# One transfer instead of two or four for keys, values and rotary queries, and another price of transfers in the layout in time

## The chip, the cores and the metric

The kernel runs on one core of one Trainium2 chip. A core has a matrix engine (PE, with its weight loads shown as PEld), a vector engine (DVE), a scalar engine (ACT), a general engine (POOL) and a queue that issues transfers (SP). The transfers themselves are carried out by 16 DMA engines of the core. The metric is the device time of one execution in microseconds (us).

## The reference, cut to what matters

One inference step of a 2-layer encoder over 2048 prompt positions and 64 sample positions. Each layer projects the input, runs four groups of heads (A: banded softmax attention; B: latent attention whose queries and keys have a rotary part of 32; C: stick-breaking attention; M: attention over 256 memory tokens), normalises and gates the heads, and projects back. The two groups that matter most here read the whole past:

```python
def mla_keys(ckv, krope, lp):                       # group B
    kv = heads(ckv @ lp['b_wkv_b'], B_HEADS)
    k_nope = rms(kv[..., :B_NOPE], lp['b_kn_g'])
    kr = jnp.broadcast_to(krope[:, :, None, :], krope.shape[:2] + (B_HEADS, B_ROPE))
    return jnp.concatenate([k_nope, kr], -1), kv[..., B_NOPE:]
...
def stick_break(q, k, v, qpos, kpos):               # group C
    z = jnp.einsum('bqhd,bkhd->bhqk', q, k).astype(jnp.float32) * Dh ** -0.5
    mask = kpos[None, :] < qpos[:, None]
    log_1m = jnp.where(mask, jax.nn.log_sigmoid(-z), 0.0)
    tail = lax.cumsum(log_1m, axis=3, reverse=True) - log_1m
    w = jnp.where(mask, jnp.exp(jax.nn.log_sigmoid(z) + tail), 0.0)
    return jnp.einsum('bhqk,bkhd->bqhd', w.astype(v.dtype), v)
```

## The kernel before, in words

The 2048 positions are 16 tiles of 128, and the sample is a 17th tile. The tiles lie in three blocks (6, 6 and 5 tiles). A stream of projections (`p_stream`) and a stream of attention (`attention`) are written alternately. Every number is split in a high and a low part, so that one product is two or three matmuls. A projected tile is transposed and stored in DRAM tensors: queries in `d["QA"]` to `d["QM"]`, rotary queries in `d["QR"]`, keys and values in `d["KVA"]`, `d["KVB"]`, `d["KVC"]` (a prompt's, in runs of 4 tiles), `d["KVM"]` and `d["KVS.."]` (memory and sample, runs of 2 tiles). The attention stream reads them back a head at a time.

`load_kv` brings the keys and values of one head and one run into the tile `kv`, whose 128 partitions hold the high part (0 to 63) and the low part (64 to 127). In DRAM these two halves lie in two halves of the tensor, so that it issues one transfer for each, of 64 rows. A full run of 4 tiles is 64 rows of 4 KB for each half; there are five `kv` buffers. `load_q` brings in the queries of a pair of tiles; for group B it also brings the rotary part `qr`, four transfers of 32 rows each, from the three copies in `d["QR"]` (the first copy twice). There is one `qr` buffer. `qr_stack` stores a tile of rotary queries: the high and low part by one transfer, a second high part by another.

Nothing is issued as it is written. A class `Plan` records each operation with its dependencies, gives it a duration (`cost`), lays all out in time (`issue`), and writes each engine's instructions in the order of the start times that it found. So the figures in `cost` decide the order on all engines, and through the buffers also when a transfer can be issued. All transfers are issued by SP, in its order; SP waits in that order too. All recorded instructions carry the line number of `issue` (L291) in the profile, so that tiles' names must tell them apart.

Of the kernel before, what the change touches and what calls it, by code (L numbers as in the profile page):

```python
# [7 lines left out]
F32 = mybir.dt.float32  # L8
F32R = mybir.dt.float32r
# [36 lines left out]
class Plan:  # L46
# [86 lines left out]
    def cost(self, eng, method, outs, ins, kw):  # L133

        def cols(x):
            n = 1
            for k in list(x.shape)[1:]:
                n *= k
            return n

        def sbuf(x):
            return "PSUM" not in str(x.space)

        n = cols(outs[0])
        if eng == "PE":
            if method == "transpose" or kw.get("rhs") is None:
                return 110, 271
            n = cols(kw["rhs"])
            return max(0.46 * n + 1, 110), 170 + 0.53 * n
        if eng == "SP":  # L150
            size = 4 * outs[0].shape[0] * n if len(outs[0].shape) > 1 else 4 * n
            return 530, 2800 + size * 0.0072
        if eng == "DVE":
            if method == "tensor_tensor_scan":
                d = 150 + 2.2 * n
            elif n <= 16:
                d = 185 + (cols(ins[0]) if method == "tensor_reduce" else 0) * 0.85
            elif len(ins) > 1 and sbuf(ins[0]) and sbuf(ins[1]):
                d = 200 + 1.35 * n
            else:  # L160
                d = 150 + 1.05 * n
            return d - 80, d
        if eng == "ACT":
            d = 190 + 0.76 * n
            if self.is_ap(kw.get("scale")):
                d += 90
            if len(outs) > 1:
                d += 230
            return d - 100, d
        if method == "memset":  # L170
            d = 100 + n
        elif kw.get("op") is not None and "pow" in str(kw["op"]):
            d = 600 if n == 1 else 1050
        elif method == "tensor_scalar":
            d = 245 + 1.3 * n
        else:
            d = 200 + 1.75 * n
        return d - 30, d
# [5 lines left out]
    def issue(self, tc):  # L184
        import heapq
        ops, tiles = self.ops, self.tiles
        n = len(ops)
# [17 lines left out]
        at = [0.0] * n  # L205
# [12 lines left out]
                        return key  # L218
            return None

        now, done = 0.0, 0
        while done < n:
            moved = False
            for e in ready:
                while clock[e] <= now and ready[e]:
                    i = heapq.heappop(ready[e])
                    key = slot(i)
                    if key is not None:
                        parked[key].append(i)
                        continue  # L230
                    for x in ops[i][5]:
                        if x not in held:
                            k = tiles[x][0]
                            held.add(x)
                            free[k] -= 1
                            turn[k] += 1
                            if turn[k] < len(order[k]) and free[k] > 0:
                                for j in parked[k]:
                                    heapq.heappush(ready[ops[j][0]], j)
                                parked[k] = []  # L240
                    take, last = ops[i][6]
                    if e == "ACT":
                        t = self.table(ops[i][3])
                        if t and t != act:
                            act = t
                            take, last = take + 1300, last + 1300
                    start[i] = now
                    clock[e] = now + take
                    heapq.heappush(events, (now + take, 0, e, i))
                    heapq.heappush(events, (now + last, 1, e, i))  # L250
                    moved = True
                    break
            if moved:
                continue
            if not events:
                raise AssertionError(("plan", done, {k: (v[:3], [ops[j][0] for j in v[:3]]) for k, v in parked.items() if v}))
            now = events[0][0]
            while events and events[0][0] <= now:
                _, kind, e, i = heapq.heappop(events)
                if kind == 0:  # L260
                    if e == "PE":
                        for j in after[i]:
                            if ops[j][0] == "PE":
                                left[j] -= 1
                                if left[j] == 0:
                                    heapq.heappush(ready["PE"], j)
                    continue
                if kind == 1:
                    done += 1
                    for x in ops[i][5]:  # L270
                        uses[x] -= 1
                        if uses[x] == 0:
                            k = tiles[x][0]
                            held.discard(x)
                            free[k] += 1
                            for j in parked[k]:
                                heapq.heappush(ready[ops[j][0]], j)
                            parked[k] = []
                    for j in after[i]:
                        if e == "PE" and ops[j][0] == "PE":  # L280
                            continue
                        heapq.heappush(events, (now + (10 if ops[j][0] == e else self.LAG[ops[j][0]]), 2, e, j))
                    continue
                left[i] -= 1
                if left[i] == 0:
                    heapq.heappush(ready[ops[i][0]], i)
# [26 lines left out]
def hybrid_step(  # L313
# [29 lines left out]
    pj = pool("pj")  # L343
    at = pool("at")
# [48 lines left out]
    def dt(name, shape, dtype=F32):  # L393
        return dram.tile(shape, dtype, name=name, tag=name)
# [5 lines left out]
    def layer_dram(l):  # L400
        d = {}
        for b, tl in enumerate(blocks):
            d["QR", b] = dt(f"qr{l}_{b}", [3, 128, len(tl) * 128])
            for g in "ABCM":
                d["Q" + g, b] = dt(f"q{g}{l}_{b}", [2, 256, len(tl) * 128])
                d["G" + g, b] = dt(f"g{g}{l}_{b}", [128, len(tl), 256])
        for g in "ABC":
            d["KV" + g] = dt(f"kv{g}{l}", [2, NH, HD, (NT + 3) // 4, 2, 512])
        for s in ("SA", "SB", "SC", "M", "SM"):
            d["KV" + s] = dt(f"kv{s}{l}", [2, NH, HD, 2, 256])  # L410
        d["KR"] = dt(f"kr{l}", [128, NT * 128])
        d["KRS"] = dt(f"krs{l}", [128, 256])
        d["Y"] = {t: dt(f"y{l}_{t}", [128, 1024]) for t in range(NT + 1)}
        D[l] = d
# [343 lines left out]
    def qr_stack(src, dst):  # L758

        pt = ps_st.tile([128, 128], F32, name="ptqr")  # L760
        T.transpose(pt, src, ident)
        kt = pj.tile([128, 2, 128], F32R, tag="qrs", name="qrs", bufs=1)
        A.copy(out=kt[:, 0], in_=pt)
        sub_r(kt[:, 1], pt, kt[:, 0])
        Y.dma_start(out=dst[0:2].rearrange("a p t -> p a t"), in_=kt.bitcast(F32))
        Y.dma_start(out=dst[2], in_=kt[:, 0].bitcast(F32))

    def v_stack(src, dst):

# [20 lines left out]
    def small_T(src, n, tag):  # L790

        pt = ps_st.tile([128, n, 128], F32, name="pts")
        for k in range(n):
            T.transpose(pt[:, k, :], src[:, k * 128:(k + 1) * 128], ident)
        h = pj.tile([128, n, 128], F32R, tag=tag + "h", name=tag + "h", bufs=1)
        lo = pj.tile([128, n, 128], F32R, tag=tag + "l", name=tag + "l", bufs=1)
        A.copy(out=h, in_=pt)
        sub_r(lo, pt, h)
        return h, lo
# [563 lines left out]
    def load_kv(d, g, h, c, n, sample):  # L1363
        kv = at.tile([128, 2, 512], F32R, tag="kv", name="kv", bufs=5)
        if sample or g == "M":
            src = d["KV" + ("S" if sample else "") + g][:, h]
        else:
            src = d["KV" + g][:, h, :, c]
        for a in range(2):
            Y.dma_start(out=kv[64 * a:64 * a + 64, :, 0:n * 128].bitcast(F32), in_=src[a, :, :, 0:n * 128])  # L1370
        return kv
# [10 lines left out]
    def group_units(l, b, g):  # L1382
# [13 lines left out]
        def load_q(p):  # L1396
# [4 lines left out]
            Y.dma_start(out=p["q"][0:64, :, 0:w].bitcast(F32), in_=src)  # L1401
            Y.dma_start(out=p["q"][64:128, 0, 0:w].bitcast(F32), in_=src[:, 0])
            if g == "B":
                p["qr"] = at.tile([128, 256], F32R, tag="qr", name="qr", bufs=1)
                for e in range(4):
                    Y.dma_start(out=p["qr"][32 * e:32 * e + 32, 0:w].bitcast(F32),
                                      in_=d["QR", b][e % 3, h * 32:(h + 1) * 32, t0:t0 + w])

        for h in range(NH):
            start = []  # L1410
# [409 lines left out]
```

## Time and profile before

| what | value |
|---|---|
| median of 3 runs | 3264.21 us (3263.85 to 3267.9) |
| profiled execution | 3270.62 us, of which the span is 3268.8 us |
| PE busy | 3136.6 us (96%) |
| DVE, ACT, POOL busy | 82%, 60%, 46% |
| moved by the DMA engines | 558.95 MB, mean 171 GB/s |

The span runs from the first instruction to the last. A busy share of PE of 96% says that PE is hardly ever without work; the shares of the other engines are averages over stages. The DMA share is an average over 16 DMA engines.

### The profile page before, as it was taken

How to read it: one execution, taken by the hardware profiler on the slowest of the kernel's cores; microseconds unless marked ns; L12 is line 12 of the kernel's file. 1: busy time of each engine (PE TensorE's matmuls, PEld its weight loads, DVE VectorE, ACT ScalarE, POOL GpSimd, SP SyncE). 2: the span in 40 equal slices, each digit the busy share in tenths (PEclk: the TensorE clock that was granted, in tenths of full speed). 3: DMA queues.
4: the chain of work that ended last, by engine and by line, in shares of the span. 5: the costliest groups of instructions: out<-in, count | busy, mean ns of one | idle time of the engine just before them, and what ended most of it. 6: DMA issues, size and time to landing. Idle time of an engine off the chain costs nothing.

```text
span 3268.8 us, 75613 instructions
## 1 busy us (share of the span) xinstructions
PE 3136.6 (96%) x24486; PEld 3004.7 (92%) x24486; DVE 2678.8 (82%) x7977; ACT 1959.3 (60%) x5336; POOL 1512.6 (46%) x2353
## 2 busy tenths in 40 slices
PE   8999989999999999999999989999999999999899
PEld 7999889999999998999999888989999998998798
DVE  5787868998889689887878977899878888887984
ACT  4455646767665565566656765666646567655650
POOL 4664445765346246442444544476313544212562
PEclk9999999999999999999999999999999999999999
DMA  6655776644656666566566667744455766566545
GB/s 187 196 153 165 198 205 196 160 120 140 169 159 194 200 184 179 150 171 179 148 187 181 173 179 218 197 138 131 137 142 166 210 197 188 158 173 175 151 129 157
DMA packets 576123, 558.95 MB, mean 171 GB/s; under 512 B 70960, under 2 KB 478000, under 8 KB 575728
## 3 DMA queue, kind: packets, MB, share of 16 engines
q1 hardware_dynamic: 575728, 554.10, 60.2%
q8 instruction: 196, 3.21, 0.4%
q14 instruction: 199, 1.63, 0.2%
HBM read 378.21 MB, written 173.75 MB: 169 GB/s over the span
## 4 chain that ended last, share of the span: by engine, by line
PE 66%; DVE 14%; DMA 8%; issue 4%; ACT 4%; POOL 2%; SPq 2%; POOLq 0%; DVEq 0%; ACTq 0%
PE pp L291 35%; PE ps L291 10%; PE ot L291 8%; PE pt L291 7%; DVE wh L291 4%; DVE r L291 3%; DVE ph L291 2%; PE ob L291 2%; SPq L291 2%; PE ptk L291 1%; ACT s L291 1%; DMA kv<-kvA 1%; PE ptq L291 1%; PE ptx L291 1%; DVE s L291 1%
## 5 line engine op out<-in xcount | busy, mean ns | idle before, releaser
L291 PE MATMUL pp<-wh,xh 128*128 128x256 f32 (+1 forms) x9104 | 1805.5, 291 | 26.1 <-ACT ev L291 10.3
L291 PEld LDWEIGHTS pp<-wh,xh 128*128 128x128 f32 x9104 | 1436.3, 190 | 61.7 <-DVE wh L291 18.6
L291 PE MATMUL pp<-wh,xl 128*128 128x256 f32 (+1 forms) x4416 | 1236.7, 281 | 2.2 <-DVE xl L291 1.9
L291 PEld LDWEIGHTS pp<-wh,xl 128*128 128x128 f32 x4416 | 838.8, 190 | 7.7 <-DVE xl L291 3.9
L291 POOL TENSOR_SCALAR wh<-raw,gc 128x256 fp32r<-128x256 f32 (+1 forms) x848 | 470.5, 570 | 355.2 <-PE pp L291 292.4
L291 ACT CAST ph<-pt 128x512 fp32r<-128x512 f32 (+2 forms) x840 | 454.2, 551 | 289.0 <-PE pt L291 276.2
L291 DVE TENSOR_TENSOR ph<-pt,ph 128x512 fp32r<-128x512 f32 (+2 forms) x840 | 523.5, 633 | 112.6 <-ACT ph L291 108.4
L291 PE MATMUL ot<-ph,kv 128*128 128x256 f32 (+1 forms) x3232 | 579.6, 289 | 6.9 <-DVE ph L291 3.2
L291 PE MATMUL ps<-kv,qbuf 128*128 128x256 f32 (+3 forms) x2048 | 541.5, 361 | 27.0 <-DVE r L291 8.8
L291 PE MATMUL pt<-identr,s 128*128 128x128 f32 x3056 | 504.1, 274 | 23.4 <-ACT s L291 11.3
L291 DVE SCALAR_TENSOR_TENSOR wh<-raw,gc,wh 128x256 fp32r<-128x256 f32 (+1 forms) x848 | 477.0, 596 | 24.6 <-POOL wh L291 21.9
L291 ACT ACTIVATE s<-s,nm 128x512 f32<-128x512 f32 (+4 forms) x600 | 383.9, 642 | 173.7 <-DVE nm L291 166.9
L291 PEld LDWEIGHTS ot<-ph,kv 128*128 128x128 f32 x3232 | 466.1, 190 | 20.4 <-DVE ph L291 5.0
L291 POOL TENSOR_TENSOR s<-s,r 128x512 f32<-128x512 f32 (+3 forms) x328 | 322.2, 984 | 248.4 <-DVE r L291 211.8
L291 POOL TENSOR_TENSOR st<-st,mhalf 128x4 f32<-128x4 f32 (+1 forms) x312 | 279.9, 903 | 274.2 <-DVE st L291 202.2
L291 PEld LDWEIGHTS pt<-identr,s 128*128 128x128 f32 x3056 | 356.3, 141 | 37.1 <-ACT s L291 14.2
L291 DVE TENSOR_TENSOR_SCAN r<-ps,r,one 128x512 f32<-128x512 f32 (+3 forms) x328 | 354.2, 1102 | 29.2 <-ACT ps L291 24.9
L291 PEld LDWEIGHTS ps<-kv,qbuf 128*128 128x128 f32 x2048 | 320.5, 190 | 55.7 <-DVE r L291 12.8
L291 ACT ACTIVATE ev<-pp,xst 128x256 f32<-128x256 f32 (+1 forms) x424 | 199.8, 472 | 259.9 <-PE pp L291 222.7
L291 POOL TENSOR_TENSOR mst<-mst,mhalf 128x4 f32<-128x4 f32 x136 | 138.9, 1027 | 255.4 <-DVE mst L291 251.9
L291 ACT ACTIVATE s<-ps 128x512 f32<-128x512 f32 (+3 forms) x328 | 165.9, 536 | 107.0 <-DVE ps L291 55.7
L291 DVE TENSOR_SCALAR_CACHE_REDUCE s<-ps 128x512 f32<-128x512 f32 (+1 forms) x328 | 182.2, 573 | 28.0 <-PE ps L291 25.6
(151 smaller groups left out, 4000.3 us busy)
## 6 DMA issues: line engine op xcount, KB each, us to landing
raw<-in_w_in SPq DMA_DIRECT2D x288, 256.0 KB, 3.4
kv<-kvC SPq DMA_DIRECT2D x128, 256.0 KB, 4.2
kv<-kvB SPq DMA_DIRECT2D x128, 256.0 KB, 4.2
kv<-kvA SPq DMA_DIRECT2D x96, 256.0 KB, 4.6
raw<-in_w_out SPq DMA_DIRECT2D x96, 256.0 KB, 3.9
y<-y SPq DMA_DIRECT2D x136, 128.0 KB, 2.7
xin<-y SPq DMA_DIRECT2D x64, 256.0 KB, 4.1
qC<-kt SPq DMA_DIRECT2D x34, 256.0 KB, 2.9
```

What stands on the lines that cost most here:

```text
L291: op[1](*op[2], **op[3])
```

## The change

Three edits. First, transfers are joined: a `kv` tile whose run is as long as the last dimension of its source (a full run of 4 tiles, or the 2 tiles of memory and sample) comes by one transfer with the halves as outermost dimension of the source; `d["QR"]` gets a fourth copy, and the rotary queries of a pair come by one transfer whose source has the four copies outermost. `qr` gets a second buffer, and the tiles of `small_T` for the latent keys and the latent queries share one buffer (their room goes to `qr`). Second, `qr_stack` stores two copies of the high part where it stored one. Third, in `Plan` a transfer holds SP for 440 ns and a part by its size in place of 530 ns, and all transfers share one wire of 4 ns a KB.

```diff
         if eng == "SP":
-            size = 4 * outs[0].shape[0] * n if len(outs[0].shape) > 1 else 4 * n
-            return 530, 2800 + size * 0.0072
+            size = 4 * n * outs[0].shape[0]
+            return 440 + size / 2048, size
...
+                    if e == "SP":
+
+                        begin = max(now + 2000, wire)
+                        wire = begin + 0.004 * last
+                        last = max(wire, now + 2000 + 0.0045 * last) - now + 300
...
-            d["QR", b] = dt(f"qr{l}_{b}", [3, 128, len(tl) * 128])
+            d["QR", b] = dt(f"qr{l}_{b}", [4, 128, len(tl) * 128])
...
-        Y.dma_start(out=dst[2], in_=kt[:, 0].bitcast(F32))
+        Y.dma_start(out=dst[2:4].rearrange("a p t -> p a t"),
+                          in_=kt[:, 0:1].bitcast(F32).to_broadcast([128, 2, 128]))
...
-        h = pj.tile([128, n, 128], F32R, tag=tag + "h", name=tag + "h", bufs=1)
-        lo = pj.tile([128, n, 128], F32R, tag=tag + "l", name=tag + "l", bufs=1)
+        h = pj.tile([128, n, 128], F32R, tag="sTh", name=tag + "h", bufs=1)
+        lo = pj.tile([128, n, 128], F32R, tag="sTl", name=tag + "l", bufs=1)
...
+        if n * 128 == src.shape[-1]:
+            Y.dma_start(out=kv.bitcast(F32)[:, :, 0:n * 128], in_=src)
+            return kv
         for a in range(2):
             Y.dma_start(out=kv[64 * a:64 * a + 64, :, 0:n * 128].bitcast(F32), in_=src[a, :, :, 0:n * 128])
...
-                p["qr"] = at.tile([128, 256], F32R, tag="qr", name="qr", bufs=1)
-                for e in range(4):
-                    Y.dma_start(out=p["qr"][32 * e:32 * e + 32, 0:w].bitcast(F32),
-                                      in_=d["QR", b][e % 3, h * 32:(h + 1) * 32, t0:t0 + w])
+                p["qr"] = at.tile([128, 256], F32R, tag="qr", name="qr", bufs=2)
+                Y.dma_start(out=p["qr"][:, 0:w].bitcast(F32),
+                                  in_=d["QR", b][:, h * 32:(h + 1) * 32, t0:t0 + w])
```

The numbers of transfers follow from the code: 352 transfers of 64 rows of 4 KB become 176 of 128 rows; 112 transfers of memory and sample become 56; 288 of rotary queries become 72. In source and destination, outermost first, a full run goes from 64 rows on both sides to 2 times 64 rows in the source and 128 rows in the destination; a pair of rotary queries goes from 32 rows on both sides to 4 times 32 rows and 128 rows.

How the order moves is seen on SP in the second block of layer 0, at the first runs of group C (`kv` from `kvC`). The rows give what is written, what is read, and the shape of what is written. Before:

```order
L291 DMA kv_2359<-kvC0_137 64x1024 x2
L291 DMA qM0_1_124<-kt_2272 128x4x128
L291 DMA gt_2360<-gA0_0_110 128x256
L291 DMA qbuf2_87<-qM0_0_115 64x2x256
L291 DMA qbuf2_87<-qM0_0_115 64x256
L291 DMA y0_3_148<-y_2294 128x256
L291 DMA qbuf0_85<-qC0_1_122 64x256
L291 DMA qbuf0_85<-qC0_1_122 64x2x256
L291 DMA raw_2384<-in_w_in 128x512
```

And after:

```order
L296 DMA kv_2359<-kvC0_137 128x1x1024
L296 DMA qM0_1_124<-kt_2272 128x4x128
L296 DMA y0_3_148<-y_2294 128x256
L296 DMA qbuf2_87<-qM0_0_115 64x2x256
L296 DMA qbuf2_87<-qM0_0_115 64x256
L296 DMA gt_2360<-gA0_0_110 128x256
L296 DMA qbuf0_85<-qC0_1_122 64x256
L296 DMA qbuf0_85<-qC0_1_122 64x2x256
L296 DMA raw_2384<-in_w_in 128x512
```

Two rows have become one, a store of `y` and a load of gates (`gt`) have changed places, and the load of `kv_2359` stands where it stood.

The second place is PE where it first reads `kv_2323`, the first of these runs (`ps` are scores, `pp` a projection, `ob` and `pt` transposes). Before:

```order
L291 MATMUL pt_2346<-identr_79,s_2325 128x128 x2
L291 MATMUL ob_2358<-identr_79,os_2330 128x128
L291 MATMUL ps_2363<-kv_2323,qbuf0_85 128x384 x2
L291 MATMUL ps_2366<-kv_2323,qbuf0_85 128x512 x2
L291 MATMUL pp_2354<-wh_2312,xh_1369 128x256
L291 MATMUL ot_2369<-ph_2347,kv_2261 128x256
```

And after:

```order
L296 MATMUL pt_2346<-identr_79,s_2325 128x128 x2
L296 MATMUL ob_2358<-identr_79,os_2330 128x128
L296 MATMUL ps_2363<-kv_2323,qbuf0_85 128x384 x2
L296 MATMUL ps_2366<-kv_2323,qbuf0_85 128x512 x2
L296 MATMUL pp_2354<-wh_2312,xh_1369 128x256
L296 MATMUL ot_2369<-ph_2347,kv_2261 128x256
```

Nothing moved here but the line number: the scores that need the run stand ahead of the next projection, as before.

The third place is SP near the start, where the caches' tail is copied from DRAM to DRAM. The line in `caches` writes 64 rows of 256 numbers. Before:

```order
L291 DMA xin_227<-in_x_prompt 128x512
L291 DMA raw_262<-in_w_in 128x512
L291 DMA o_aks<-in_ca_k 16x1024
L291 DMA o_avs<-in_ca_v 16x1024
L291 DMA bt_1482<-in_bias_p 128x640
```

And after:

```order
L296 DMA trig_323<-in_c_trig 128x64
L296 DMA o_aks<-in_ca_k 16x1024
L296 DMA o_avs<-in_ca_v 16x1024
L296 DMA raw_262<-in_w_in 128x512
L296 DMA raw_263<-in_w_in 128x512
```

The copies have moved one load of weights ahead. In both programs the 64 contiguous rows stand as 16 rows of 1024.

## Rows read from the trace of the kernel before

**Rows 1.** The page's busy times: engine, busy us, share, instructions

```profile
PE 3136.6 (96%) x24486; PEld 3004.7 (92%) x24486; DVE 2678.8 (82%) x7977; ACT 1959.3 (60%) x5336; POOL 1512.6 (46%) x2353
```

**Rows 2.** PE's waits that a transfer ended: us in total, times, longest us

```profile
PE ps L291 <- DMA qr<-qr: 9.0, 11, 1.6
...
PE ps L291 <- DMA kv<-kvC: 1.3, 1, 1.3
...
PE ps L291 <- DMA kv<-kvA: 0.6, 1, 0.6
```

**Rows 3.** The DMA queues over the whole span: packets, MB, share of 16 engines

```profile
q1 hardware_dynamic: 575728, 554.10, 60.2%
```

**Rows 4.** Issues of the transfers concerned, whole span: count, KB each, median us to landing

```profile
kv<-kvC SPq DMA_DIRECT2D x128, 256.0 KB, 4.2
kv<-kvB SPq DMA_DIRECT2D x128, 256.0 KB, 4.2
kv<-kvA SPq DMA_DIRECT2D x96, 256.0 KB, 4.6
...
qr<-qr SPq DMA_DIRECT2D x256, 32.0 KB, 2.2
...
kv<-kvM SPq DMA_DIRECT2D x48, 128.0 KB, 2.8
...
kv<-kvSC SPq DMA_DIRECT2D x16, 128.0 KB, 3.6
...
qr<-qr SPq DMA_DIRECT2D x32, 16.0 KB, 2.0
```

**Rows 5.** DMA queues from 893.0 to 893.4 us, the start of a kv load

```profile
DMA packets 15, 0.06 MB, mean 154 GB/s; under 512 B 0, under 2 KB 0, under 8 KB 15
...
q1 hardware_dynamic: 15, 0.06, 40.0%
```

**Rows 6.** DMA queues from 892.9 to 897 us, both halves of that load

```profile
DMA packets 152, 0.48 MB, mean 118 GB/s; under 512 B 34, under 2 KB 34, under 8 KB 152
...
q1 hardware_dynamic: 152, 0.48, 41.9%
```

**Rows 7.** Issues that touch tile kv: ns min/median/max, first and last start in us

```profile
L291 SPq DMA_DIRECT2D kv<-kvC x144: 444/586/1689, 141.6 to 3128.1; - x144
```

**Rows 8.** Busy times by stretch; the last three columns are clock, DMA share, GB/s

```profile
0.00:141.60 141.60, 125.02 (x924) 117.83 (x924) 89.30 (x287) 58.56 (x170) 76.78 (x149) 0.99 0.67 191
141.60:3128.10 2986.50, 2877.93 (x22479) 2756.54 (x22480) 2503.16 (x7523) 1865.35 (x5089) 1377.98 (x2120) 0.99 0.61 171
3128.10:3268.80 140.70, 133.69 (x1084) 130.31 (x1082) 86.32 (x169) 35.37 (x78) 57.80 (x84) 0.98 0.48 146
```

**Rows 9.** DMA queue and issues from 1450 to 1600 us

```profile
q1 hardware_dynamic: 28599, 23.07, 56.2%
...
kv<-kvB SPq DMA_DIRECT2D x24, 256.0 KB, 4.1
...
qr<-qr SPq DMA_DIRECT2D x20, 32.0 KB, 2.0
...
kv<-kvSB SPq DMA_DIRECT2D x4, 128.0 KB, 3.4
...
qr<-qr SPq DMA_DIRECT2D x12, 16.0 KB, 2.4
```

**Rows 10.** DMA queue and issues from 163 to 490 us

```profile
q1 hardware_dynamic: 68965, 58.54, 63.7%
...
kv<-kvB SPq DMA_DIRECT2D x8, 256.0 KB, 4.2
kv<-kvA SPq DMA_DIRECT2D x8, 256.0 KB, 5.1
...
qr<-qr SPq DMA_DIRECT2D x44, 32.0 KB, 2.2
...
kv<-kvC SPq DMA_DIRECT2D x3, 256.0 KB, 5.9
```

**Rows 11.** Busy times from 31 to 35.5 us; columns as in the stretches above

```profile
31.00:35.50 4.50, 3.21 (x12) 2.96 (x13) 2.16 (x7) 2.29 (x5) 1.62 (x3) 0.62 0.44 127
```

More of the change, by code (lines that the diff above doesn't have):

```diff
@@ L219, in slot @@
             return None
-        now, done = 0.0, 0
+        now, done, wire = 0.0, 0, 0.0
         while done < n:
```

## The prediction

> **What bounds the kernel now.** The busy times come first: PE works 3136.6 of 3268.8 us, so 132 us are all that could be gained by taking every wait from it [rows 1]. Next, which of its waits a transfer ends: 9.0 us for rotary queries in 11 waits, 1.3 us for the runs of group C, 0.6 us for those of A [rows 2]. So the transfers that the change joins are hidden almost entirely behind PE's other work. Third, how full the DMA engines are: packets of the one hardware queue took 60.2% of 16 engines' span, which is 1968 us on each engine, and moved 554.10 MB, 34.6 MB on each [rows 3]. That is 17.6 GB/s for one engine while it is busy. PE is the bound, and the DMA engines have 40% to spare so long as the bytes lie evenly on all 16.
>
> **The change: fewer issues.** SP issues 448 transfers fewer and 34 of them larger (the second high part of the rotary queries). The median issue of a kv transfer holds SP 586 ns [rows 7]; all 448 would be 263 us, but of SP, and nothing on PE is seen to wait for an issue of these beyond the some 11 us of the waits above. The second `qr` buffer takes away those 9.0 us at the most. Together I count at most 20 us of gain.
>
> **The layout in time.** The order shown of SP and PE hardly moves: one store past one load, and none of PE's instructions. I take 0 with 20 us to both sides, since PE's 132 us idle are the only room for a gain. The shared buffer of `small_T` makes ACT's copy wait for the few matmuls of the other user; ACT is idle for 40% of the span [rows 1], so it costs nothing. Without that cover it would be some 70 waits of under 2 us.
>
> **How a joined transfer lies on the engines.** This decides. Now both sides of a full run count 64 rows outermost, so 16 engines can take 4 packets of 4 KB each. Two such halves together moved at 118 GB/s over 4.1 us that include start and end, at a share of 41.9% [rows 6], which no single engine of 17.6 GB/s could do. After the change the source counts 2 outermost, the destination 128. If work is dealt out by rows of the outermost dimension, a run falls on 2 engines, 64 packets of 4 KB on each, and rotary queries on 4 engines. If it is dealt out by packets, nothing changes. No transfer of the program before has fewer than 16 rows outermost, so no row decides it. What leans to dealing by the outermost count is the program itself: the copies of 64 contiguous rows stand in it as 16 rows of 1024 (third place of the order), and there is no use in that form unless the outermost count is what is shared out among 16 engines. I take the joined transfer to be confined.
>
> The Trainium skill, page "DMA: Bandwidth & Descriptors", section "Why a DMA increments its semaphore by 16 and not by 1", says so outright: the number of engines is the largest, up to 16, that divides the outermost counts of both sides, and a hardware-issued transfer then uses the lowest-numbered ones. By that rule it is 2 engines for keys and values and 4 for rotary queries, always the same ones; no run here shows it yet. The same page's "Rules for kernel authors" advises the opposite edit for two halves of the partitions, one transfer of 128 partitions, because halves share the engines anyway; that would make the change harmless, and it is the rival of an even spread below.
>
> **What the low engines then carry.** The price of a 4 KB packet: at the start of a load 15 packets took 40.0% of 16 engines in 0.4 us, 171 ns each [rows 5]; over both halves, with all engines reading at once, 41.9% of 16 engines in 4.1 us less some 10 ns for each of the 34 small packets, over 118 packets, 230 ns each [rows 6]. So an engine moves 24.0 GB/s at best and 17.8 when crowded; the mean over the span was 17.6. Both ends, for one of the two lowest engines:
> - full runs: 352 issues of 256 KB [rows 4] become 176, each with 64 packets on each of the two: 11,264 packets, 1.93 ms at 171 ns, 2.59 ms at 230;
> - memory and sample: 48 issues from `kvM` and 16 from each of four sample tensors [rows 4] become 56, 128 KB on each engine: 7.3 MB, 0.31 to 0.42 ms;
> - rotary queries: 256 issues of 32 KB and 32 of 16 KB [rows 4] are 8.9 MB on four engines, 2.2 MB each: 0.09 to 0.13 ms;
> - all else, 554.1 less 92.3, 14.7 and 8.9 MB, plus 2.2 MB of new stores, is 440.4 MB over 16 engines, 27.5 MB: 1.15 to 1.56 ms.
>
> The sum is 3.47 to 4.70 ms, against 1.97 now: over the present span at either end. The low engines take PE's place as the bound. I take the runs at 171 ns, because only two engines read them at once (1.93), and the rest at the middle of its ends (1.83), 3.76 ms in all.
>
> By the page's section "Specifications", with some 27 GiB/s for an engine, a half of a run would take 9.0 us and all of them 1.59 ms, an estimate; the row above makes it 10.9 us.
>
> **From work to time.** The first run is loaded at 141.6 us and the last at 3128.1 [rows 7]. The 282 us outside keep their time; the engines are busy 67% and 48% of them, 162 us [rows 8]. What lies between takes 3.76 less 0.16, 3.60 ms, where it took 2.99: 3.88 ms together. The load is uneven too. From 1450 to 1600 us, 24 issues are 12 runs, 131 us; with four of the sample (13), rotary queries (10) and 15.4 MB of the rest on 16 engines (47) a low engine has 201 us of work in 150 [rows 9]. From 163 to 490 us, 19 issues are 9.5 runs, 104 us, with 18 of rotary queries and 52.1 MB of the rest (160): 282 us in 327, so 45 us go unused [rows 10]. I count as much again for other slack stretches: 3.97 ms. Landings are the other loss: a run landed 4.2 us after its issue [rows 4], now 10.9 us at least and more behind another. SP issues in order, so loads queue behind any wait for a buffer, and PE's scores stand ahead of the next projection (second place of the order), so the projections wait with them. All transfers on 16 engines, weights and stores too, now end with the slowest engine. I add 2% for rings that run dry in such waits, an estimate: **4050 us**. The profiled execution took 3270.62 us, 1.8 over its span and 6.4 (0.2%) over the median, which is less than the rounding of these sums. Between two versions of this kernel 0.2% is about what a measurement can tell from no change.
>
> **The rivals.**
> - *Even spread.* Transfers are dealt out by packets, and the change does what its code says. Then at most 20 us come off, with 20 us either way for the order: about 3250 us, within 3230 to 3285. The 16-row form of the copies speaks against it; the absence of any row with a small outermost count leaves it open. Chance 0.11: 0.06 faster, 0.04 the same, 0.01 slower.
> - *Confined, but cheap.* All packets move at 24 GB/s, since the other 14 engines are now idle for more than half the time: 3.47 ms of work, some 3.6 ms with the slack of the ends, to 3.8. For it, crowding is what separates 171 from 230 ns; against it, the mean over the span is at the crowded price. Chance 0.17.
> - *Confined and crowded, with a slow PE.* At 230 ns the work is 4.70 ms. And where PE rests its clock falls: from 31 to 35.5 us it worked 3.21 of 4.5 us at a granted clock of 0.62 of full speed, a mixture of its levels of 1.2 and 2.4 GHz [rows 11]; with a wait of microseconds at each of 232 joined loads much of the attention would run so. 4.4 to 4.9 ms. Chance 0.15.
>
> **How the numbers follow.** Confined at the mixed price, 3.8 to 4.4 ms: chance 0.57, predicted time 4050. The even spread (0.11) lies alone far below, so I leave it out, with some of the tails of the others: 3550 to 4750 holds the rest. Added up: faster 0.06, the same 0.04, slower 0.90.
>
> **What would show it.** Right: a joined run of 512 KB lands in 13 us or more (64 packets at 171 ns, and the 2 us that the smallest transfers take [rows 4]), where a half took 4.2; the DMA share over the span falls below 55%, since 14 engines idle; PE's busy share falls to about 80% with waits for `kv` in hundreds of us, longest in stretches like 1450 to 1600, and the first 140 us hardly change. Weight loads and stores, whose form is the same, land later too. Wrong: a run lands in 4 to 6 us, and PE stays at 96%. The size is wrong if packets of 4 KB take other than 171 ns, or if buffers run dry more than I count.

## The result and the profile after

| | before | changed |
|---|---|---|
| median | 3266.06 us (3263.85 to 3268.12, 4 runs) | 4489.85 us (4478.39 to 4492.83, 4 runs) |
| ratio | 1 | 1.3739, 95% interval 1.3718 to 1.3759 |
| span of the profiled execution | 3268.8 us | 4487.4 us |
| mean granted clock of PE | 0.992 | 0.874 |

The change makes the kernel 37% slower. The forecast was 4050 us within 3550 to 4750.

The page's busy times after the change, beside [rows 1]:

```profile
PE 3438.4 (77%) x24486; PEld 3262.7 (73%) x24486; DVE 2684.4 (60%) x7977; ACT 1961.9 (44%) x5336; POOL 1499.8 (33%) x2353
```

PE executes as many instructions as before. It is busy 302 us longer, with its clock lower, and idle 1049 us where it was idle 132. The other engines work as long as before; they only wait more.

The DMA part of the page, beside [rows 3], and the issues of the runs, beside [rows 4]:

```profile
DMA packets 569190, 561.08 MB, mean 125 GB/s; under 512 B 59680, under 2 KB 471072, under 8 KB 568800
...
q1 hardware_dynamic: 568800, 556.29, 40.5%
...
kv<-kvC SPq DMA_DIRECT2D x64, 512.0 KB
kv<-kvB SPq DMA_DIRECT2D x64, 512.0 KB
kv<-kvA SPq DMA_DIRECT2D x48, 512.0 KB
```

The bytes are the same but for the 2.2 MB of new stores, and the mean share fell from 60.2% to 40.5%. That is not relief. The same row of the page before counts this many small packets:

```profile
DMA packets 576123, 558.95 MB, mean 171 GB/s; under 512 B 70960, under 2 KB 478000, under 8 KB 575728
```

Under 512 B there are 70,960 packets before and 59,680 after, 11,280 fewer. If every transfer posts one small packet on each engine that it uses, to say that it is done there, then 3579 transfers on 16 engines post 57,264, and 2827 on 16, 72 on 4 and 232 on 2 engines post 45,984. The difference is 11,280, to the packet. Were the joined loads still on 16 engines, 448 transfers fewer would post 7,168 packets fewer; a kernel below that has just as many transfers does so. The joined loads lie on 2 and 4 engines.

One such load can be seen alone. The next fence is SP's timeline from 2386 to 2409 us (start, us, engine, operation, tiles, count); the second is the DMA queue from 2400.9 to 2404.9 us, and the third the busy times of that stretch, columns as in [rows 8]:

```profile
2389.86 0.51 SPq L296 DMA_DIRECT2D kv<-kvC  x1
2391.76 0.86 SPq L296 DMA_DIRECT2D qbuf<-qC  x1
2392.72 0.54 SPq L296 DMA_DIRECT2D y<-y  x1
2393.35 0.59 SPq L296 DMA_DIRECT2D qbuf<-qC  x1
2394.03 0.87 SPq L296 DMA_DIRECT2D gM<-ev  x1
2394.95 1.29 SPq L296 DMA_DIRECT2D gt<-gA  x1
2396.34 1.16 SPq L296 DMA_DIRECT2D kv<-kvC  x1
2397.60 8.38 SPq L296 DMA_DIRECT2D qbuf<-qC  x2
2406.03 1.21 SPq L296 DMA_DIRECT2D kv<-kvC  x2
```

```profile
DMA packets 52, 0.21 MB, mean 53 GB/s; under 512 B 0, under 2 KB 0, under 8 KB 52
...
q1 hardware_dynamic: 52, 0.21, 12.9%
```

```profile
2400.90:2404.90 4.00, 0.00 (x0) 0.00 (x0) 0.00 (x0) 0.00 (x0) 0.00 (x0) 0.51 0.13 53
```

The second load of `kv` in that list, at 2396.34, is half of a partial run of 128 KB, which still comes in two loads. For 4 us the whole core does nothing but move 52 packets of 4 KB. A share of 12.9% of 16 engines is 2.06 engines, and the price is 0.129 x 16 x 4 us / 52 = 159 ns a packet. The granted clock is 0.51, near the lower of its two levels. PE's timeline shows how long the stop was:

```profile
2396.93 0.48 PE L296 MATMUL ps<-kv,qbuf 128*128 128x256 f32 x2
2407.23 0.58 PE L296 MATMUL ot<-ph,kv 128*128 128x256 f32 x1 [9.81 <-ACT os L296]
```

The completions of transfers, which the trace records with their times, show what the load does to others. Each of the seven transfers issued behind it has 14 of its 16 completions by 2401.15 us. Their last two come from 2405.60 to 2408.31, after the load's own two at 2405.38 and 2405.50. By these times every one of them waited for the two engines that the load held. The load itself landed 15.6 us after its issue.

On the other engines, waits for transfers whose form did not change grew with it. These are two of the largest, before and after (us in total, times, longest):

```profile
ACT y L291 <- DMA y<-y: 36.9, 20, 6.1
POOL fo L291 <- DMA up<-fo: 55.5, 17, 12.5
```

```profile
ACT y L296 <- DMA y<-y: 288.0, 53, 19.8
POOL fo L296 <- DMA up<-fo: 215.3, 20, 31.2
```

SP's list shows a second thing. SP issued the load at 2389.86, seven transfers behind it, and then stood still. This is SP's waits from 2386 to 2410 us (us in total, times, longest):

```profile
SPq L296 <- DMA kv<-kvC: 6.6, 1, 6.6
```

SP waits for the very load that it issued eight transfers earlier. The program gives its transfers eight semaphores in turn (the 57,264 completions before fall on eight, 7168 or 7152 on each), so a transfer is not issued before the eighth before it has landed. Over the whole span SP's waits for runs were 8.5 us or less for each group in the kernel with split loads (below). After the change they are as follows; the first row is a store, on 16 engines:

```profile
SPq L296 <- DMA x<-xr: 142.2, 34, 11.8
...
SPq L296 <- DMA kv<-kvC: 110.0, 29, 7.0
SPq L296 <- DMA kv<-kvA: 103.7, 32, 7.2
SPq L296 <- DMA kv<-kvB: 97.5, 31, 6.7
```

### The profile page after: what moved, and what is told of

The parts are those of the page before. It is cut to its first block, busy times and chain, and to the rows that moved or that the text cites. A ratio compares the mean times of both kernels' runs of the same rounds, so it can differ in the third digit from the quotient of the medians.

```text
span 4487.4 us, 75073 instructions
## 1 busy us (share of the span) xinstructions
PE 3438.4 (77%) x24486; PEld 3262.7 (73%) x24486; DVE 2684.4 (60%) x7977; ACT 1961.9 (44%) x5336; POOL 1499.8 (33%) x2353
## 2 busy tenths in 40 slices
DMA packets 569190, 561.08 MB, mean 125 GB/s; under 512 B 59680, under 2 KB 471072, under 8 KB 568800
## 3 DMA queue, kind: packets, MB, share of 16 engines
q1 hardware_dynamic: 568800, 556.29, 40.5%
## 5 line engine op out<-in xcount | busy, mean ns | idle before, releaser
L296 PE MATMUL pp<-wh,xh 128*128 128x256 f32 (+1 forms) x9104 | 1916.6, 304 | 101.7 <-ACT ev L296 57.2
L296 PEld LDWEIGHTS pp<-wh,xh 128*128 128x128 f32 x9104 | 1542.9, 203 | 142.8 <-ACT ev L296 59.9
L296 PE MATMUL pp<-wh,xl 128*128 128x256 f32 (+1 forms) x4416 | 1288.2, 293 | 2.1 <-DVE xl L296 1.6
L296 PE MATMUL ps<-kv,qbuf 128*128 128x256 f32 (+3 forms) x2048 | 612.1, 395 | 474.4 <-DMA kv<-kvC 87.1
L296 PEld LDWEIGHTS pp<-wh,xl 128*128 128x128 f32 x4416 | 894.1, 203 | 7.7 <-DVE xl L296 4.0
L296 PEld LDWEIGHTS ps<-kv,qbuf 128*128 128x128 f32 x2048 | 361.1, 213 | 521.9 <-issue 287.9
L296 PE MATMUL ot<-ph,kv 128*128 128x256 f32 (+1 forms) x3232 | 621.2, 304 | 102.4 <-ACT os L296 41.3
L296 PE MATMUL pt<-identr,s 128*128 128x128 f32 x3056 | 533.5, 287 | 85.8 <-ACT s L296 23.9
L296 PEld LDWEIGHTS ot<-ph,kv 128*128 128x128 f32 x3232 | 503.8, 205 | 123.7 <-ACT os L296 44.0
L296 PEld LDWEIGHTS pt<-identr,s 128*128 128x128 f32 x3056 | 377.1, 147 | 101.2 <-ACT s L296 27.5
```

The lines of the kernel that those rows point to most:

```text
L296: op[1](*op[2], **op[3])
```

## The experiments

All ratios are to the kernel before, run beside each on the same chip. Its medians there were 3265 to 3266 us, so times of different experiments can be compared to a few us.

**Loads split again.** The joined loads of the changed kernel are taken back; the new prices, the second `qr` buffer and the fourth copy stay.

```diff
-        if n * 128 == src.shape[-1]:
-            Y.dma_start(out=kv.bitcast(F32)[:, :, 0:n * 128], in_=src)
-            return kv
...
-                Y.dma_start(out=p["qr"][:, 0:w].bitcast(F32),
-                                  in_=d["QR", b][:, h * 32:(h + 1) * 32, t0:t0 + w])
+                for e in range(4):
+                    Y.dma_start(out=p["qr"][32 * e:32 * e + 32, 0:w].bitcast(F32),
+                                      in_=d["QR", b][e, h * 32:(h + 1) * 32, t0:t0 + w])
```

> All joined loads are split again (two loads for keys and values, four for rotary queries); the new prices in the layout, the second rotary buffer and the fourth copy stay. If the loss comes from joined loads lying on 2 and 4 engines, as predicted: 3235 to 3285 us, DMA packets under 512 B up again by 11,280 less 34 times 0 (the stores are as many as before). If the new prices or the new order lose time: over 3300 us.

3252.28 us, ratio 0.9963 (95% interval 0.995 to 0.9976). The whole loss is gone, and the rest of the change gains 14 us. SP's waits in this kernel:

```profile
SPq L296 <- DMA x<-xr: 37.6, 26, 3.6
...
SPq L296 <- DMA kv<-kvA: 8.5, 15, 1.5
...
SPq L296 <- DMA kv<-kvC: 4.6, 7, 0.8
...
SPq L296 <- DMA kv<-kvB: 3.9, 8, 1.1
```

Its packets under 512 B are 70,960 again. It is the base of what follows.

**Only the rotary queries joined.** As the changed kernel, without the three lines for `kv`.

> Only the rotary queries are joined (72 loads whose source counts 4 outermost); keys and values come in two loads each. If it is the work of the low engines that counts: engines 0 to 3 get 0.1 ms on top of some 1.9 ms, far under the span, so 3235 to 3295 us. If every confined load costs a fixed delay (1224 us over 304 of them, 4.0 us each): 72 of them add 290 us, 3550 us.

3257.69 us, 0.9975 (0.9966 to 0.9984): 5 us over the base for 72 loads on 4 engines, with 32 packets of 1 KB on each; the two intervals overlap. The fixed delay of 4 us for any confined load is refuted; small ones are almost wholly hidden.

**The same transfers, 128 rows at one step.** The source of a joined load is replaced; its size, its number and its place stay.

```diff
         if n * 128 == src.shape[-1]:
+            e = min(h, 2)
...
+                src = d["KV" + g][0, e:e + 2, :, c]
-            Y.dma_start(out=kv.bitcast(F32)[:, :, 0:n * 128], in_=src)
+            Y.dma_start(out=kv.bitcast(F32)[:, :, 0:n * 128], in_=src.rearrange("h p b t -> (h p) b t"))
```

> As the changed kernel, with as many and as large transfers, but the source of each joined load is 128 rows at one step (the high parts of two neighbouring heads in place of the high and low part of one; for rotary queries the high part of all four heads), so that the outermost count is 128 on both sides. It leaves out that the right numbers are loaded. If the outermost count of 2 or 4 is the cause: 3230 to 3290 us. If a transfer of 512 KB in one piece, or the layout in time, is the cause: 4300 us or more.

3227.85 us, 0.9887 (0.9872 to 0.9903). Neither the size of a transfer nor the layout in time is to blame. On 16 engines joined loads cost nothing: with the joined rotary queries this kernel is 24 us faster than the base. It has 7,168 small packets fewer than the kernel before, 16 for each of the 448 transfers saved. And a run of twice the size lands about as fast as a half did in [rows 4]:

```profile
DMA packets 573302, 561.10 MB, mean 174 GB/s; under 512 B 63792, under 2 KB 475184, under 8 KB 572912
...
kv<-kvC SPq DMA_DIRECT2D x64, 512.0 KB, 4.4
kv<-kvB SPq DMA_DIRECT2D x64, 512.0 KB, 4.3
kv<-kvA SPq DMA_DIRECT2D x48, 512.0 KB, 4.9
```

**Half of the heads.** The base, with `kv` joined where `h % 2 == 0`: 88 full runs and 28 loads of memory and sample.

> Keys and values are joined for every second head only, rotary queries split. If the sum of work on the two low engines is the bound: they carry about 2.9 ms (1.5 of common traffic, 0.95 of 88 full runs, 0.2 of memory and sample, 0.2 of split runs), less than the span of 3.27, so most of it is hidden and the time is 3300 to 3550 us, far less than half of the loss. If each confined load costs a fixed delay, half of the loss stays: 3880 us.

3881.9 us, 1.1897 (1.1868 to 1.1926). This is just half of the loss. The sum over the span, on which the forecast rested, is refuted: by the estimate above the low engines carry 2.9 ms of work, less than the span is long, and the loss is there all the same.

**Odd runs.** The base, with `kv` joined where `c % 2 == 1`. Within a head the joined runs then lie apart.

> As the kernel with all loads split, but the full runs with an odd number are joined: 64 runs on 2 engines, at most one of three or two of four of a head, and never two neighbouring ones. The half-and-half kernel lost as much for each joined load as the changed one (5.4 and 5.3 us), where whole heads were joined. If a joined load delays by its own late landing, whatever is beside it, the price stays: 64 times 5.3 to 7 us, 3590 to 3700 us. If the two low engines are the bound only where joined loads lie close together, they have room here (two runs of 10.8 us and 30 us of common traffic in a head of 60 us) and most of the price goes: 3260 to 3400 us.

3708.76 us, 1.1356 (1.134 to 1.1371): 456 us over the base for 64 runs, 7.1 us each. That is just over the upper of the two forecasts. It is also the price in the other two: 630 us over 88 full runs are 7.2, and 1238 us over 176 are 7.0. There the loads of memory and sample are counted at nothing, which the odd runs allow: they cost as much each, with no such load joined. So a full run costs 7 us on average in all three choices of runs. The bound in stretches, the second form of my theory, falls too.

**Four and eight engines.** The kernel with 128 rows at one step, but with rows taken in 4 groups of 32 or 8 of 16 (for 4: `in_=src[:, 0:32]` of all four heads).

> The kernel with 128 rows at one step, but the rows of keys and values are taken as 4 groups of 32 rows, so that the source counts 4 outermost (the rows are again not the right ones; rotary queries at one step). A run then is 32 packets on each of 4 engines, 5.4 us. If the price is what the landing (about 2 us and the packets) has over the some 11 us of head start that loads have now: nearly nothing, 3230 to 3400 us. If the price is the time that the low engines hold up everything behind the load, it halves: 3228 plus 620, 3850 us.

3693.85 us, 1.1306 (1.1281 to 1.133).

> The same with 8 groups of 16 rows: 16 packets on each of 8 engines, 2.7 us. Price of the landing alone: 3228 to 3260 us. Price in proportion to the time on the low engines: 3228 plus 310, 3540 us. If the number of engines were not what counts, 3228 or 4490.

3365.02 us, 1.0293 (1.027 to 1.0316).

Over the 3228 us on 16 engines a full run loses 2.6 us on 4 engines (466 / 176) and 0.8 on 8 (137 / 176), and 7.2 on 2 (1262 / 176). At 159 ns a packet the run takes 10.2 us on 2 engines, 5.1 on 4, 2.5 on 8 and 1.3 on 16. So 65 to 81% of the time by which the engines are held longer than on 16 comes back as loss. The landing alone (at most 3400 us on 4 engines) is refuted. The price in proportion expected 3850 and 3540 us, so 622 and 312 us of loss. Measured are 466 and 137: it was too high by a third on 4 engines, and more than twice too high on 8. Part of the miss is that it left out the time for which a run holds the engines on 16 too.

**Extra copies that nobody waits for.** The base, with a copy of each odd run from DRAM to DRAM, its source with 2 outermost.

```diff
             Y.dma_start(out=kv[64 * a:64 * a + 64, :, 0:n * 128].bitcast(F32), in_=src[a, :, :, 0:n * 128])
+        if n * 128 == src.shape[-1] and c % 2 == 1:
+            rot["scr"] = rot.get("scr", 0) + 1
+            Y.dma_start(out=dt(f"scr{rot['scr']}", [2, 64, 2, 512]), in_=src)
```

> All loads split as in the first experiment; in addition, right behind each of the 64 odd runs, a copy of that run from DRAM to a scratch tensor of its own in DRAM, 512 KB with 2 outermost, which nobody reads or waits for. If a joined run costs time by what it holds up behind it on the low engines: the price of 7.1 us each is there without anyone waiting for the run itself, up to 3252 plus 456, 3550 to 3710 us. If it costs time by its own late landing alone: 3252 to 3300 us.

3784.92 us, 1.1595 (1.1572 to 1.1619).

> The same 64 extra copies of 512 KB, with 128 rows at one step as source (another head's rows), so that they lie on 16 engines. It shows what the extra bytes cost by themselves. Both theories: 3252 to 3290 us; if it is as slow as the extra copies on 2 engines, it is the bytes and not the engines.

3314.58 us, 1.0155 (1.0136 to 1.0175). The bytes cost 62 us over the base, more than the 38 that were allowed for; lying on 2 engines costs 470 more, 7.3 for each copy. No operation needs these copies, so the price of a run on 2 engines can be paid entirely by what stands behind it. SP waits for these copies too (41.1, 27.7 and 26.3 us for the three groups). Who waits on the other engines is a list of stores that give a buffer back and of small loads (engine, tile, what ended the wait: us, times, longest):

```profile
POOL vs L296 <- DMA kvC<-vs: 144.1, 15, 33.9
POOL vs L296 <- DMA kvB<-vs: 98.9, 9, 58.8
ACT ev L296 <- DMA gC<-ev: 97.5, 9, 32.7
POOL fo L296 <- DMA up<-fo: 89.1, 20, 24.2
```

In the control on 16 engines these four are 38.6, 33.5, 6.8 and 51.5 us. SP is held in one more way here: the issue of a copy itself can last long. These are the copies from `kvB` on 2 engines, and then in the control (shortest, median and longest issue in ns):

```profile
L296 SPq DMA_DIRECT2D scr<-kvB x24: 604/652/9747, 425.2 to 3023.1; - x24
```

```profile
L296 SPq DMA_DIRECT2D scr<-kvB x24: 476/588/704, 433.3 to 2628.2; - x24
```

**A queue of its own.** The 64 odd runs on 2 engines, issued by ACT, and as a control the same with 128 rows at one step.

```diff
+    Z = plan.engine("SP", nc.scalar)
...
-            Y.dma_start(out=kv.bitcast(F32)[:, :, 0:n * 128], in_=src)
+            Z.dma_start(out=kv.bitcast(F32)[:, :, 0:n * 128], in_=src)
```

> The 64 odd runs joined on 2 engines as before (3709 us), but issued by ACT, so that they stand in a queue of their own on the same engines. If what counts is that SP's later transfers wait behind a run in SP's queue, most of the 456 us go: 3300 to 3450 us. If the run's own late landing counts: 3650 us or more. Waits for buffers now stand in ACT's order; the next kernel shows what that costs.

3726.5 us, 1.1407 (1.1386 to 1.1428).

> The same with the 64 runs as 128 rows at one step, on 16 engines (not the right rows), issued by ACT: what the issue by ACT costs by itself. 3240 to 3330 us by both theories.

3261.41 us, 0.9989 (0.9976 to 1.0003). Issue by ACT costs about nothing, and the own queue saves nothing: 465 us over its control, 7.3 a run. The idea that it is the order in SP's own queue that makes the loss is refuted. Two sets of rows show why. This is the DMA part from 1541.7 to 1545.7 us of the kernel with runs issued by ACT (`q10` is that queue):

```profile
DMA packets 89, 0.24 MB, mean 60 GB/s; under 512 B 15, under 2 KB 15, under 8 KB 89
...
q1 hardware_dynamic: 57, 0.11, 9.2%
q10 hardware_dynamic: 32, 0.13, 8.5%
```

Again fewer than 3 of 16 engines work (17.7%). On them 32 packets of the run passed in 4 us, where 52 passed in the stretch above, with 57 packets of SP's transfers, 15 of them small, in between. From 1544.1 to 1545.7 us of it both queues moved equally many packets:

```profile
q10 hardware_dynamic: 14, 0.06, 8.8%
q1 hardware_dynamic: 14, 0.03, 4.6%
```

So the queues share the low engines packet by packet, 4 KB of the run against 2 KB of SP's transfers. The run itself is longer under way, and SP's transfers still pass beside it at one packet a turn. And SP's waits for runs in this kernel:

```profile
SPq L296 <- DMA kv<-kvC: 163.6, 25, 11.2
SPq L296 <- DMA kv<-kvA: 130.0, 20, 13.0
SPq L296 <- DMA kv<-kvB: 127.4, 25, 13.5
```

All completions fall on the same eight semaphores here too, so both queues share them. SP waits 421 us for runs, where it waited 262 with the same runs in its own queue. So this kernel takes away the order in SP's queue, but not SP's stop at the eighth transfer.

**The right rows on 16 engines.** Keys and values are laid out in DRAM so that high and low part of a head adjoin (heads by parity, pair, part, row), and one load takes 128 rows at one step. A store of keys becomes two of 64 rows.

```diff
-            d["KV" + g] = dt(f"kv{g}{l}", [2, NH, HD, (NT + 3) // 4, 2, 512])
+            d["KV" + g] = dt(f"kv{g}{l}", [2, 2, 2, HD, (NT + 3) // 4, 2, 512])
...
+            for e in range(2):
+                Y.dma_start(out=dst[e].rearrange("i a p t -> p (i a) t"),
+                                  in_=kt[64 * e:64 * e + 64].bitcast(F32).rearrange("p i a t -> p (i a) t"))
...
+            src = d["KV" + g][h % 2, h // 2, :, :, c]
+        Y.dma_start(out=kv[:, :, 0:n * 128].bitcast(F32), in_=src.rearrange("a p b t -> (a p) b t")[:, :, 0:n * 128])
```

> The right rows on all 16 engines: the DRAM tensors of keys and values are laid out anew, so that high and low part of a head lie next to each other and one load takes 128 rows at one step, partial runs too; a store of keys is two transfers of 64 rows for one of 128, and rotary queries are loaded split. The kernel with rows at one step took 3228 us and the split one 3252, so if the joined load on 16 engines is what gained those 24 us: 3225 to 3250 us. If the joined rotary queries gained them, or the further stores take them back: 3250 to 3275 us.

3252.11 us, 0.9949 (0.9936 to 0.9963). That is the second of the two forecasts: the joined load by itself gained nothing, or the further stores took it back. It beats the kernel before by 0.5%, as the split base does by 0.4%; between the two there is no difference that these intervals show. What the 3228 us of the kernel with rows at one step have over both, the joined rotary queries or the fewer stores, was not separated.

## Why the prediction was right, and where it was not

**Confinement.** Right, and the step that decided. The outermost count is what is shared out: 2 engines for runs, 4 for rotary queries, by the count of small packets and by the kernel that differs in the step of rows alone. The Trainium skill, page "DMA: Bandwidth & Descriptors", section "Why a DMA increments its semaphore by 16 and not by 1", has this rule, and the 11,280 packets agree with it. Which of the 16 engines they are, no row here tells. The advice of the Trainium skill, the same page's "Rules for kernel authors", for halves of the partitions is one transfer of 128, the edit made here; it cost nothing once the rows lay at one step (0.9887 and 0.9949). The two sentences meet in the source's shape: the one transfer was harmless with 128 rows outermost in the source, and cost time with 8, 4 or 2.

**Price of a packet.** I took 171 ns for the runs, where [rows 5, 6] gave 171 and 230; alone on the two engines it was 159. A smaller price, so the error to low is not from here.

**From work to time.** This is the step that was mis-sized. The forecast allowed 0.29 ms beyond the 3.76 ms of work on the two low engines; measured were 4.49 ms, 0.73 beyond it. The reasoning behind the term was wrong as well: with 88 or 64 of the runs joined, the work fits in the span by the estimate, and time is lost all the same. The runs showed a price of 7 us for each full run in place of it. While a run occupies two engines for 10 us, every transfer on 16 engines waits for its share on these two, and SP itself stops at the eighth transfer behind. The forecast held this in one sentence ("end with the slowest engine") and gave it 2%, a term that no run shows.

That 4490 us still lies within the range is in part luck. It lies above the 3.8 to 4.4 ms of the case that was held likeliest, and the sum of work, from which the range was built, doesn't set the time.

How the 7 us divide is left open: among SP's wait at the eighth transfer, the late ends of the others, and issues that hold SP. All three are in the rows. A kernel with more semaphores in turn would tell the first from the second and was not tried. Long issues come and go at the same price:

```profile
L291 SPq DMA_DIRECT2D raw<-in_w_out x96: 327/339/1339, 1096.0 to 3238.2; - x96
```

```profile
L296 SPq DMA_DIRECT2D raw<-in_w_out x96: 327/383/13646, 1355.3 to 4457.0; - x96
```

Before, the longest issue of these loads of weights was 1.3 us, and in the changed kernel it is 13.6. With the runs issued by ACT it is 1.0, and a run costs 7.3 us all the same.

**The rivals.** The even spread is refuted. The time fell where the crowded rival stood (4.4 to 4.9 ms), but not for its reason: packets were cheap. Its other half, the clock, was right in kind: PE is busy 302 us longer for the same instructions at a mean clock of 0.874. How much of these 302 us lies on the path was not measured.

**The signs.** The load seen alone landed 15.6 us after its issue (13 or more were expected), the mean DMA share is 40.5% (below 55), PE is busy 77% (about 80). PE waits 200 us for runs, beside 1.9 in [rows 2]:

```profile
PE ps L296 <- DMA kv<-kvC: 87.1, 16, 7.5
...
PE ps L296 <- DMA kv<-kvA: 57.1, 7, 11.9
PE ps L296 <- DMA kv<-kvB: 55.6, 13, 7.4
```

That is a fifth of PE's added idle time; the rest is put down to other transfers and other engines.

**What was costed at little or nothing.** Fewer issues, second buffer and order were given at most 20 us of gain, with 20 either way; 14 us of gain were measured for the rest of the change, without the joined loads. The start kept its time as counted: the first 141.6 us have 126.63 us of PE's work, beside 125.02 in [rows 8]:

```profile
0.00:141.60 141.60, 126.63 (x924) 118.73 (x924) 90.24 (x287) 58.50 (x170) 76.87 (x149) 0.98 0.66 192
```

## What to carry to other kernels

Before joining transfers, write down the outermost count of both sides: a leading 2 or 4 in the source puts all bytes on as many engines, and the fix is a layout in which the joined rows lie at one step. Don't price such a load by the sum of bytes on the busiest engine alone: every other transfer ends on that engine too, and an issuing queue that reuses a few semaphores in turn stops behind it. Here, with PE busy 96% before, each load cost 65 to 81% of the further time for which it held its engines. A mean DMA share that falls while the time rises is the sign to look for.

## What the runs showed that was not expected

The cost of a run on 2 engines was the same 7 us with 64, 88 and 176 of them, and 7.3 for copies that nobody reads. A second issuing queue shares the engines packet by packet: the run's packets fell from 52 to 32 in 4 us, and nothing was won. The eight semaphores in turn are a hidden depth of SP's queue: 311 us of waits for runs in the changed kernel, 17 in the base. And an issue of 0.4 us at the median held SP for up to 13.6 us in the changed kernel; why it lasts is not shown.
